# A top-k threshold search: its bits searched directly, and one secant search for four blocks instead of two for two

## The chip, the cores and the metric

One NeuronCore of a Trainium2 chip runs the whole program. The metric is device time in microseconds (us); the median of three runs is 2239.26 us. The engines are TensorE (PE: matmuls; PEld: its weight loads), VectorE (DVE), ScalarE (ACT), GpSimd (POOL) and the queue that issues nearly all DMAs (SP).

## The reference

A trunk of two layers over 2048 tokens of width 1024. The first layer has sparse attention beside a depthwise convolution of 31 taps; the second is a gated short convolution. What the change touches is the choice of keys in the sparse attention:

```python
for each block of 128 queries t:
    score = sum_h w[q, h] * relu(qi[q, h] . ki[s])      # 8 index heads
    score = where(s <= t, score, -inf)
    _, sel = top_k(score, 256)                          # 256 keys of each query
    p = softmax(q . k[sel] / 8 over valid sel);  out = p @ v[sel]
```

The kernel needs no list of the 256 keys. It needs, for each query row, a threshold such that 256 scores reach it; it then adds a mask of 0 or -1e30 to the logits.

## The kernel before, in words

The tokens are four chunks of 512 (numbered 0 to 3), and a chunk is four blocks of 128 queries (16 blocks in all, numbered 0 to 15). Block b has scores of width W = (b+1)*128. Blocks 0 and 1 need no search. A compile-time scheduler lays out each engine's instruction order; an engine then runs its list in that order. Program order is the scheduler's priority; `weave` mixes filler work (convolution, first attention) into matmul units.

Part one of the program runs, for each chunk c, `project(c)` (query and key projections), then `index` (the scores: TensorE into `ps_i`, ScalarE relu at L721, VectorE multiply-add into the score tile at L723, eight heads in columns of up to 1024), then the search. Between them lie `rest(c)` (the other projections and gates) as TensorE filler.

Blocks 2 and 3 (chunk 0) are searched exactly by `general`, called by `select_all`: 32 counts (L292) for each of the two blocks, one bit of the threshold at a time, with small VectorE operations on 128x2 tiles between them (L293 to L295, L301 to L304).

Chunks 1 to 3 use `select`, twice a chunk: blocks 0 and 1 of the chunk (pair A below) once their scores are there, then blocks 2 and 3 (pair B). `select` makes seven trips: ScalarE counts the scores above x (L774, one count a block), then a chain of ten small VectorE operations on 128x2 tiles (L778 to L789) moves x by the secant rule. Then the extraction: VectorE counts once more (L799), masks (L804), takes the best 16 scores below x (L730 to L732), picks the threshold (L812, L813) and writes the mask (L817). L821 notes rows that the search couldn't settle in `bad`.

The score tiles `sc0` to `sc3` have one buffer each, so `index` of block i of the next chunk waits until the extraction of block i of this chunk is done.

After chunk 3, `bad` is reduced to a flag (`fl`, L967; `fi`, L971), which every engine loads (L1133) ahead of an `If` that holds the exact search as a fallback, and that isn't taken here. Nothing that stands behind the `If` in the program can pass it: the rest of attention, the second layer. Ahead of it TensorE has `rest(3)`, the last gates (`last_gates`, tiles `yh`, `yl`) and the first output projection (`out_even`).

Of the kernel before, what the change touches and what calls it, by code (L numbers as in the profile page):

```python
# [12 lines left out]
FP32 = mybir.dt.float32  # L13
F16 = mybir.dt.float16
BF16 = mybir.dt.bfloat16
I32 = mybir.dt.int32
AF = mybir.ActivationFunctionType
ALU = mybir.AluOpType
# [3 lines left out]
P = 128  # L22
# [6 lines left out]
TT = CH // P  # L29
# [5 lines left out]
TOPK = 256  # L35
# [7 lines left out]
NCAND = 16  # L43
# [30 lines left out]
def trunk_kernel(ctx: ExitStack, tc: tile.TileContext, xT, pos, wE, woE, wO, woO, par, tab, outT):  # L74
    nc = tc.nc
    V, A, G, T, SP = nc.vector, nc.scalar, nc.gpsimd, nc.tensor, nc.sync
# [197 lines left out]
    def general(scs, get):  # L274
        bl = sorted(scs)
        nb, wmax = len(bl), (bl[-1] + 1) * P

        def small(name, dt=FP32):
            return get(name, TT, dt)[:, 0:nb]

        cur, tr, bits, xm, acc = small("cur", I32), small("try", I32), small("bits", I32), small("xm", I32), small("acc", I32)
        cnt, cg, tmp, zero, izero = small("cnt"), small("cg"), small("tmp"), small("zero"), small("izero", I32)
        V.memset(cg, 0.0)
        V.memset(zero, 0.0)
        V.memset(izero, 0)
        V.memset(xm, 0x7FFFFFFF)
        V.memset(cur, -2 ** 31)

        def count(th):
            for n, b in enumerate(bl):  # L290
                junk = get("junk", wmax, BF16)
                V.tensor_scalar(out=junk[:, 0:(b + 1) * P], in0=scs[b], scalar1=th[:, n:n + 1], scalar2=0.0, op0=ALU.is_ge, op1=ALU.add, accum_out=cnt[:, n:n + 1])  # L292
            V.tensor_scalar(out=acc, in0=cnt, scalar1=float(TOPK), scalar2=None, op0=ALU.is_ge)  # L293
            V.scalar_tensor_tensor(out=tmp, in0=cnt, scalar=float(TOPK), in1=cnt, op0=ALU.is_lt, op1=ALU.mult)
            V.tensor_tensor(out=cg, in0=cg, in1=tmp, op=ALU.max)  # L295

        count(zero)
        V.copy_predicated(out=cur, mask=acc, data=izero)
        V.copy_predicated(out=xm, mask=acc, data=izero)
        for bit in range(30, -1, -1):  # L300
            V.tensor_scalar(out=tr, in0=cur, scalar1=1 << bit, scalar2=None, op0=ALU.bitwise_or)  # L301
            V.tensor_tensor(out=bits, in0=tr, in1=xm, op=ALU.bitwise_xor)
            count(bits.bitcast(FP32))
            V.copy_predicated(out=cur, mask=acc, data=tr)  # L304
        V.tensor_tensor(out=bits, in0=cur, in1=xm, op=ALU.bitwise_xor)
        thr = bits.bitcast(FP32)
        V.tensor_scalar(out=cg, in0=cg, scalar1=-1.0, scalar2=float(TOPK), op0=ALU.mult, op1=ALU.add)
        for n, b in enumerate(bl):
            W = (b + 1) * P
            both, mb = get("eq", wmax, FP32), get("mb", wmax, BF16)[:, 0:W]  # L310
            eq, cs = both[:, 0:W], both[:, wmax:wmax + W]
            V.tensor_scalar(out=eq, in0=scs[b], scalar1=thr[:, n:n + 1], scalar2=None, op0=ALU.is_equal)
            V.tensor_tensor_scan(out=cs, data0=ones[:, 0:1].broadcast_to([P, W]), data1=eq, initial=0.0, op0=ALU.mult, op1=ALU.add)
            V.scalar_tensor_tensor(out=eq, in0=cs, scalar=cg[:, n:n + 1], in1=eq, op0=ALU.is_gt, op1=ALU.mult)
            V.scalar_tensor_tensor(out=eq, in0=scs[b], scalar=thr[:, n:n + 1], in1=eq, op0=ALU.is_lt, op1=ALU.add)
            V.tensor_scalar(out=mb, in0=eq, scalar1=NEG, scalar2=None, op0=ALU.mult)
            SP.dma_start(out=mb_dr[b], in_=mb)
# [90 lines left out]
    with ExitStack() as es:  # L408
# [6 lines left out]
        tk = es.enter_context(tc.tile_pool(name="tk", bufs=2))  # L415
# [285 lines left out]
        def index(c, qst, blocks):  # L701
            scs = {}
            first = cvp.tile([P, NJ, CH], FP32, name="cv") if c == 0 else None
            for i in blocks:
                b = c * TT + i
                W = (b + 1) * P
                if c == 0:
                    sc = first[:, i, 0:W]
                else:
                    sc = scp.tile([P, W], FP32, name=f"sc{i}", padded_shape=[P, (NB - TT + i + 1) * P])  # L710
                sm = tk.tile([P, 2], FP32, name=f"sm{i}")
                for sgi, s0 in enumerate(range(0, W, 1024)):
                    w = min(1024, W - s0)
                    for h in range(H):
                        ps = ps_i.tile([P, 1024], FP32, name="ps_i")
                        for r0 in range(0, w, 512):
                            r = min(512, w - r0)
                            for a in range(2):
                                T.matmul(out=ps[:, r0:r0 + r], lhsT=qst[:, h, i * P:(i + 1) * P], rhs=ki[:, a, s0 + r0:s0 + r0 + r], start=a == 0, stop=a == 1)  # L719
                        rl = e1.tile([P, 1024], FP32, name="relu")  # L720
                        A.activation(out=rl[:, 0:w], in_=ps[:, 0:w], func=AF.Relu)  # L721
                        kw = {"accum_out": sm[:, sgi:sgi + 1]} if h == H - 1 else {}
                        V.scalar_tensor_tensor(out=sc[:, s0:s0 + w], in0=rl[:, 0:w], scalar=wi[:, b, h:h + 1],  # L723
                                               in1=tiny[:, s0:s0 + w] if h == 0 else sc[:, s0:s0 + w],
                                               op0=ALU.mult, op1=ALU.add, **kw)
                scs[b] = (sc, sm, W)
            return scs
# [6 lines left out]
        def select(c, scs):  # L734
            bl = sorted(scs)
            nb, b0 = len(bl), bl[0]

            def small(name, dt=FP32, bufs=2):
                return tk.tile([P, 2], dt, name=name, bufs=bufs)[:, 0:nb]

            mu, sg, sq = small("t_mu"), small("t_sg"), small("t_sq")
            for n, b in enumerate(bl):
                sc, sm, W = scs[b]
                junk = tk.tile([P, S], BF16, name="junk", bufs=1)
# [24 lines left out]
            for it in range(NCOUNT):  # L769
                cn, d, t, xn = small("t_cn"), small("t_d", bufs=4), small("t_1"), small("t_x", bufs=4)  # L770
                for n, b in enumerate(bl):
                    sc, sm, W = scs[b]
                    junk = tk.tile([P, S], BF16, name="junk", bufs=1)
# [15 lines left out]
                V.tensor_tensor(out=xn, in0=x, in1=g if it > 0 else t, op=ALU.add)  # L789
                xl, dl, x = x, d, xn  # L790

            cand = tk.tile([P, 2, NCAND + 1], FP32, name="t_cand")
            cn, Tt, Tn, j, j1 = small("t_cn"), small("t_T"), small("t_Tn"), small("t_j"), small("t_j1")
            pick = tk.tile([P, NCAND + 1], FP32, name="t_pick")
            slot = tab_sb[:, TAB_IDX:TAB_IDX + NCAND + 1]
# [110 lines left out]
        acc = stats(0, held)  # L906
# [18 lines left out]

        def scan(c, xs):
            qst = project(c, xs)
            select(c, index(c, qst, (0, 1)))
            select(c, index(c, qst, (2, 3)))

        a, b, d = score_slot(3, 4), score_slot(0, 3), score_slot(1, 3)
        held = [a[:, k, :] for k in range(4)] + [b[:, k, :] for k in range(3)] + [d[:, 0, :]]
# [2 lines left out]
        acc = stats(1, held)  # L935
        state["gate"] = None
        qst = project(0, xs)
# [161 lines left out]
    def rows():  # L1099
        return l1.tile([P, KD, CH], FP32, name="x1"), l1.tile([P, CH], FP32, name="ssum", bufs=1)  # L1100
# [17 lines left out]
    x1, acc = rows()  # L1118
# [9 lines left out]
    n = norm_odd(x1, acc, late)  # L1128
# [4 lines left out]
    with tc.If(rv > 0):  # L1133
        with tc.tile_pool(name="fb", bufs=1) as fb:
            for c in range(1, NCH):
                scs = {}
                for i in range(TT):
                    b = c * TT + i
# [40 lines left out]
    for c in range(NCH):  # L1179
        att = attend(c + 1) if c + 1 < NCH else iter(())  # L1180
        if c > 0:
            cnv = conv(c + 1) if c + 1 < NCH else iter(())
            x1, acc = rows()
            weave(out_even(c, *m[c], x1, acc), 99, (cnv, CNR), (att, R0))
            n = norm_odd(x1, acc, late, (cnv, CNR), (att, R1))
# [78 lines left out]
```

## Time and profile before

| what | value |
|---|---|
| median of the runs shown (2239.11 to 2239.54) | 2239.26 us |
| the profiled execution | 2238.43 us |
| its span in the trace | 2236.6 us |
| TensorE busy in the span | 1992.6 us (89%) |
| VectorE busy | 1677.2 us (75%) |
| ScalarE busy | 1119.3 us (50%) |
| GpSimd busy | 773.8 us (35%) |

The profiled execution is 1.8 us longer than its span. Times in the trace count from the start of the span. A matmul's record is longer than the step from one matmul to the next, since matmuls overlap in the array; the busy figures count overlapping records once.

### The profile page before, as it was taken

What the parts mean: (1) busy time and instruction counts of PE and PEld (TensorE: products, weight loads), DVE (VectorE), ACT (ScalarE), POOL (GpSimd) and SP (SyncE); (2) the same over time, 40 slices, a digit from 0 to 9 for tenths busy, and PEclk for the clock granted to TensorE, in tenths of its full rate; (3) what the DMA queues carried; (4) which work ended last, traced back from release to release, by engine and by line L of the source; (5) the groups of instructions that cost most, each with busy time, mean ns of one, the idle gap of its engine ahead of it and who ended that gap; (6) DMA issues with size and microseconds to landing.
All of it is one profiled execution on the core that took longest, in us unless ns stands there. A gap on an engine that the chain in (4) does not pass through costs nothing.

```text
span 2236.6 us, 34187 instructions
## 1 busy us (share of the span) xinstructions
PE 1992.6 (89%) x12252; PEld 1070.5 (48%) x12252; DVE 1677.2 (75%) x3568; ACT 1119.3 (50%) x1899; POOL 773.8 (35%) x633
## 2 busy tenths in 40 slices
PE   5777888988999898798889998989998989999997
PEld 4544464555454543344444444544554444444446
DVE  7999979999887876778875899763899874243224
ACT  5556655567568756366664553451555463121111
POOL 4755343534142502246552543430444442000000
PEclk9989999999999998899989999999999999999999
DMA  6445456334744466678886787773778976324224
GB/s 237 160 157 192 164 172 228 111 115 139 222 127 151 130 227 212 205 208 206 199 211 190 174 202 188 179 182 121 184 173 190 207 159 162 118 101 147 96 97 167
DMA packets 408094, 380.85 MB, mean 170 GB/s; under 512 B 315504, under 2 KB 335728, under 8 KB 387184
## 3 DMA queue, kind: packets, MB, share of 16 engines
q1 hardware_dynamic: 407920, 378.64, 59.5%
q8 instruction: 96, 1.57, 0.3%
q14 instruction: 78, 0.64, 0.1%
HBM read 216.45 MB, written 88.70 MB: 136 GB/s over the span
## 4 chain that ended last, share of the span: by engine, by line
PE 24%; DVE 13%; DMA 8%; issue 5%; ACT 4%; POOL 3%; SPq 1%; POOLq 0%; DVEq 0%; ACTq 0%
PE ps_w L189 7%; PE ps_w L188 7%; PE ps_w L187 7%; DVE lg L340 3%; DVE ps_c L241 3%; DMA w_stage<-in_wo_dram 2%; DMA pth<-ph 2%; POOL pl L351 2%; DMA ptl<-pl 1%; ACT ph L350 1%; DMA cin<-cg_dr 1%; DVE y L1060 1%; ACT lg L343 1%; POOL wt L210 1%; DVE nl L183 1%
## 5 line engine op out<-in xcount | busy, mean ns | idle before, releaser
L351 POOL TENSOR_TENSOR pl<-lg,ph 128x1024 f16<-128x1024 f32 (+7 forms) x192 | 317.1, 1664 | 562.3 <-ACT ph L350 444.5
L187 PE MATMUL ps_w<-nh,wt 128*128 128x512 f16 x1024 | 389.1, 382 | 6.8 <-ACT wt L209 4.6
L189 PE MATMUL ps_w<-nh,wt 128*128 128x512 f16 x1024 | 388.4, 382 | 3.6 <-POOL wt L210 3.5
L188 PE MATMUL ps_w<-nl,wt 128*128 128x512 f16 x1024 | 390.1, 382 | 1.4 <-DVE nl L183 1.4
L187 PEld LDWEIGHTS <-wt 128*128 128x128 f16 x2112 | 208.6, 99 | 258.7 <-issue 24.1
L189 PEld LDWEIGHTS <-wt 128*128 128x128 f16 x2112 | 208.8, 99 | 245.3 <-issue 16.0
L188 PEld LDWEIGHTS <-wt 128*128 128x128 f16 x2112 | 209.0, 99 | 242.4 <-issue 27.3
L241 DVE SCALAR_TENSOR_TENSOR ps_c<-cin,cwt,ps_c 128x512 f32<-128x512 f32 x348 | 260.2, 748 | 20.1 <-ACT ps_c L239 17.1
L210 POOL TENSOR_TENSOR wt<-w_stage,wt 128x512 f16<-128x512 f32 x136 | 167.9, 1241 | 285.8 <-ACT wt L209 260.5
L343 ACT ACTIVATE lg<-lg,m 128x128 f32<-128x128 f32 (+15 forms) x128 | 153.5, 1199 | 136.7 <-DVE m L340 132.1
L187 PE MATMUL ps_p<-xh,wt 128*128 128x512 f16 x480 | 186.2, 389 | 16.3 <-ACT th L222 4.5
L350 ACT CAST ph<-lg 128x1024 f16<-128x1024 f32 (+7 forms) x192 | 148.2, 792 | 95.1 <-DMA pth<-ph 93.4
L189 PE MATMUL ps_p<-xh,wt 128*128 128x512 f16 x480 | 185.7, 389 | 2.1 <-POOL wt L210 2.1
L188 PE MATMUL ps_p<-xl,wt 128*128 128x512 f16 x480 | 186.1, 388 | 0.0
L721 ACT ACTIVATE relu<-ps_i 128x1024 f32<-128x1024 f32 (+7 forms) x176 | 140.9, 811 | 75.5 <-DVE sc L723 42.8
L723 DVE SCALAR_TENSOR_TENSOR sc<-relu,wi,sc 128x1024 f32<-128x1024 f32 (+7 forms) x140 | 162.3, 1160 | 13.2 <-ACT relu L721 12.4
L719 PE MATMUL ps_i<-ki,qst 128*128 128x512 f16 (+3 forms) x608 | 145.3, 361 | 26.7 <-ACT relu L721 26.3
L187 PE MATMUL ps_p<-wt,xh 128*128 128x256 f16 (+1 forms) x608 | 164.8, 271 | 4.6 <-ACT u L578 2.4
L188 PE MATMUL ps_p<-wt,xh 128*128 128x256 f16 (+1 forms) x608 | 164.6, 271 | 0.6 <-POOL wt L210 0.6
L189 PE MATMUL ps_p<-wt,xl 128*128 128x256 f16 (+1 forms) x608 | 163.9, 271 | 1.2 <-DVE xl L473 1.2
L1156 PE MATMUL ps_q<-kk,qs_a 128*128 128x512 f16 (+3 forms) x576 | 146.8, 356 | 12.2 <-DVE m L340 11.9
L774 ACT ACTIVATE junk<-sc,t_x 128x640 bf16<-128x640 f32 (+5 forms) x84 | 118.7, 1413 | 58.1 <-DVE t_x L789 34.2
(294 smaller groups left out, 3989.8 us busy)
## 6 DMA issues: line engine op xcount, KB each, us to landing
wt<-w_in_wo_dram SPq DMA_DIRECT2D x48, 1024.0 KB, 5.0
wt<-w_in_we_dram SPq DMA_DIRECT2D x39, 1024.0 KB, 5.4
w_stage<-in_wo_dram SPq DMA_DIRECT2D x64, 256.0 KB, 3.3
w_in_wo_dram<-wt SPq DMA_DIRECT2D x16, 1024.0 KB, 4.9
wt<-w_in_woo_dram SPq DMA_DIRECT2D x16, 1024.0 KB, 4.8
w_in_we_dram<-wt SPq DMA_DIRECT2D x13, 1024.0 KB, 4.8
w_stage<-in_we_dram SPq DMA_DIRECT2D x48, 256.0 KB, 3.4
wt<-w_in_woe_dram SPq DMA_DIRECT2D x12, 1024.0 KB, 4.8
```

What stands on the lines that cost most here:

```text
L187: T.matmul(out=out, lhsT=sh(k), rhs=mh(k), start=k == 0, stop=False)
L188: T.matmul(out=out, lhsT=sh(k), rhs=ml(k), start=False, stop=False)
L189: state["mm"] = T.matmul(out=out, lhsT=sl(k), rhs=mh(k), start=False, stop=k == KD - 1)
L210: G.tensor_tensor(out=wt[:, 1, ks, :], in0=st, in1=wt[:, 0, ks, :], op=ALU.subtract)
L241: ins = V.scalar_tensor_tensor(out=out if t == CK - 1 else acc, in0=ci[:, t:t + CH], scalar=cwt[:, j, t:t + 1], in1=acc, op0=ALU.mult, op1 ...
L343: A.activation(out=lg[:, 0:W], in_=lg[:, 0:W], func=AF.Exp, bias=last, scale=-1.0, accum_out=ss[:, h:h + 1])
L350: A.copy(out=ph, in_=e)
L351: eng.tensor_tensor(out=pl, in0=e, in1=ph, op=ALU.subtract)
L719: T.matmul(out=ps[:, r0:r0 + r], lhsT=qst[:, h, i * P:(i + 1) * P], rhs=ki[:, a, s0 + r0:s0 + r0 + r], start=a == 0, stop=a == 1)
L721: A.activation(out=rl[:, 0:w], in_=ps[:, 0:w], func=AF.Relu)
L723: V.scalar_tensor_tensor(out=sc[:, s0:s0 + w], in0=rl[:, 0:w], scalar=wi[:, b, h:h + 1], in1=tiny[:, s0:s0 + w] if h == 0 else sc[:, s0:s0 ...
L1156: ins = T.matmul(out=ps[:, 0:w], lhsT=qs[:, h, :], rhs=kk[:, a, s0:s0 + w], start=a == 0, stop=a == 1)
```

## The change

`general`: the threshold's own bits are searched. `cur` starts at all ones (or at zero where 256 scores are at least zero), and each bit is flipped by an exclusive-or, so that the operation that turned bits into a number (L302) goes. The running maximum of counts below 256 (L294, L295, after every count) goes too; one count with "greater than" at the end gives it instead.

`select`: it is called once a chunk with all four blocks. Its small tiles are four columns wide instead of two, and `t_cand` has one buffer instead of two.

```diff
-            V.scalar_tensor_tensor(out=tmp, in0=cnt, scalar=float(TOPK), in1=cnt, op0=ALU.is_lt, op1=ALU.mult)
-            V.tensor_tensor(out=cg, in0=cg, in1=tmp, op=ALU.max)
-        count(zero)
-        V.copy_predicated(out=cur, mask=acc, data=izero)
-        V.copy_predicated(out=xm, mask=acc, data=izero)
+            V.copy_predicated(out=cur, mask=acc, data=data)
+        count(zero, cnt, ALU.is_ge)
+        keep(izero)
         for bit in range(30, -1, -1):
-            V.tensor_scalar(out=tr, in0=cur, scalar1=1 << bit, scalar2=None, op0=ALU.bitwise_or)
-            V.tensor_tensor(out=bits, in0=tr, in1=xm, op=ALU.bitwise_xor)
-            count(bits.bitcast(FP32))
-            V.copy_predicated(out=cur, mask=acc, data=tr)
-        V.tensor_tensor(out=bits, in0=cur, in1=xm, op=ALU.bitwise_xor)
-        thr = bits.bitcast(FP32)
+            V.tensor_scalar(out=tr, in0=cur, scalar1=1 << bit, scalar2=None, op0=ALU.bitwise_xor)
+            count(tr.bitcast(FP32), cnt, ALU.is_ge)
+            keep(tr)
+        thr = cur.bitcast(FP32)
+        count(thr, cg, ALU.is_gt)
...
-                return tk.tile([P, 2], dt, name=name, bufs=bufs)[:, 0:nb]
+                return tk.tile([P, TT], dt, name=name, bufs=bufs)[:, 0:nb]
...
-            cand = tk.tile([P, 2, NCAND + 1], FP32, name="t_cand")
+            cand = tk.tile([P, TT, NCAND + 1], FP32, name="t_cand", bufs=1)
...
             qst = project(c, xs)
-            select(c, index(c, qst, (0, 1)))
-            select(c, index(c, qst, (2, 3)))
+            select(c, index(c, qst, range(TT)))
```

## Rows read from the trace of the kernel before

**Rows 1.** The page's first part: engines, busy time and share.
```profile
PE 1992.6 (89%) x12252; PEld 1070.5 (48%) x12252; DVE 1677.2 (75%) x3568; ACT 1119.3 (50%) x1899; POOL 773.8 (35%) x633
```
**Rows 2.** Windows by stage: stretch, its length, then busy us of each engine.
```profile
100.00:283.00 183.00, 146.96 (x897) 85.67 (x896) 176.94 (x526) 115.16 (x213) 93.67 (x94) 0.92 0.49 169
...
587.00:799.00 212.00, 193.34 (x1212) 108.87 (x1211) 178.76 (x389) 154.68 (x233) 67.92 (x67) 1.00 0.49 142
...
820.00:868.00 48.00, 36.87 (x157) 15.74 (x155) 13.77 (x72) 38.05 (x46) 4.58 (x4) 0.86 0.70 241
868.00:926.00 58.00, 54.64 (x256) 24.58 (x254) 53.56 (x87) 24.35 (x42) 19.73 (x16) 1.00 0.57 193
```
**Rows 3.** Waits of TensorE, 100 to 283 us: total, times, longest.
```profile
PE ps_t L613 <- DVE stk L600: 14.6, 4, 5.6
...
PE ps_t L613 <- DVE stk L606: 3.2, 3, 2.4
```
**Rows 4.** Timeline of VectorE at the flag: start, us, instruction, idle before.
```profile
925.25 0.16 DVE L967 TENSOR_REDUCE fl<-bad 128x1 f32<-128x16 f32 x1
...
933.75 0.45 DVE L147 TENSOR_TENSOR rs_t<-rs_r 128x4 f32<-128x4 f32 x1 [5.17 <-DVEq L1133]
```
**Rows 5.** Waits of TensorE, 926 to 940 us.
```profile
PE ps_m L169 <- DVE rs_d L163: 10.1, 1, 10.1
```
**Rows 6.** Groups by line, whole span: xcount, busy us, mean ns, idle before.
```profile
L292 DVE TENSOR_SCALAR_CACHE_REDUCE mk<-cv,s_bits 128x384 bf16<-128x384 f32 (+1 forms) x62 | 41.9, 676 | 1.1
...
L781 DVE SCALAR_TENSOR_TENSOR t_d<-t,t_d 128x2 f32<-128x2 f32 x42 | 12.6, 301 | 0.8
...
L302 DVE TENSOR_TENSOR s_bits<-s_try,s_xm 128x2 int32<-128x2 int32 x31 | 8.8, 285 | 0.5
...
L294 DVE SCALAR_TENSOR_TENSOR s_tmp<-s_cnt 128x2 f32<-128x2 f32 x32 | 7.9, 247 | 0.0
L295 DVE TENSOR_TENSOR s_cg<-s_cg,s_tmp 128x2 f32<-128x2 f32 x32 | 7.8, 242 | 0.0
...
L785 DVE RECIPROCAL t_g<-t_g 128x2 f32<-128x2 f32 x36 | 5.8, 162 | 0.7
```
**Rows 7.** Groups by line on VectorE, 820 to 868 us, the last search.
```profile
L780 DVE TENSOR_TENSOR t<-t_d 128x2 f32<-128x2 f32 x7 | 1.1, 161 | 0.2
```
**Rows 8.** Groups by line and shape on ScalarE, whole span: the counts.
```profile
L774 ACT ACTIVATION_READ_ACCUMULATOR junk<-sc,t_x 128x1 f32 x84 | 15.9, 189 | 0.0
L774 ACT ACTIVATE junk<-sc,t_x 128x2048 bf16<-128x2048 f32 x7 | 14.0, 1998 | 0.1
...
L774 ACT ACTIVATE junk<-sc,t_x 128x1152 bf16<-128x1152 f32 x7 | 8.8, 1252 | 6.9 <-DVE t_x L764 4.1 <-DVE t_x L789 2.7
```
**Rows 9.** Timeline of VectorE: the slot of block 8 freed, block 12 begun.
```profile
585.29 0.81 DVE L817 TENSOR_SCALAR mb<-sc,t_T 128x1152 bf16<-128x1152 f32 x1
...
587.09 1.27 DVE L723 SCALAR_TENSOR_TENSOR sc<-relu,wi,tiny 128x1024 f32<-128x1024 f32 x1
```
**Rows 10.** Windows of L723 alone: the multiply-adds of chunks 2 and 3.
```profile
346.00:522.00 176.00, 65.67 (x71) 0.95 0.43 138
...
587.00:799.00 212.00, 78.85 (x72) 1.00 0.49 142
```
**Rows 11.** Groups by line, 587 to 799 us, ScalarE: the counts among the index work.
```profile
L774 ACT ACTIVATE junk<-sc,t_x 128x1408 bf16<-128x1408 f32 (+3 forms) x28 | 45.5, 1626 | 20.5 <-DVE t_x L789 12.7 <-DVE t_x L764 5.3 <-DVE rs_t L148 2.4
```
**Rows 12.** The same stretch on VectorE: two of ten search lines.
```profile
L787 DVE TENSOR_TENSOR t_g<-t_g,t_gmin 128x2 f32<-128x2 f32 x12 | 5.1, 427 | 0.2
...
L785 DVE RECIPROCAL t_g<-t_g 128x2 f32<-128x2 f32 x12 | 1.9, 162 | 0.3
```
**Rows 13.** Groups by line on VectorE, 868 to 926 us: work beside the last extraction.
```profile
L241 DVE SCALAR_TENSOR_TENSOR ps_c<-cin,cwt,ps_c 128x512 f32<-128x512 f32 x23 | 17.1, 744 | 0.0
...
L1016 DVE SCALAR_TENSOR_TENSOR x<-ps_w,xi 128x512 f32<-128x512 f32 x8 | 5.4, 676 | 4.4 <-DMA xi<-in_x_dram 4.4
L179 DVE TENSOR_TENSOR ssum<-ssum,sq 128x512 f32<-128x512 f32 x7 | 5.1, 723 | 0.0
```

More of the change, by code (lines that the diff above doesn't have):

```diff
@@ L279, in small @@
             return get(name, TT, dt)[:, 0:nb]
-        cur, tr, bits, xm, acc = small("cur", I32), small("try", I32), small("bits", I32), small("xm", I32), small("acc", I32)
-        cnt, cg, tmp, zero, izero = small("cnt"), small("cg"), small("tmp"), small("zero"), small("izero", I32)
-        V.memset(cg, 0.0)
+        cur, tr, acc = small("cur", I32), small("try", I32), small("acc", I32)
+        cnt, cg, zero, izero = small("cnt"), small("cg"), small("zero"), small("izero", I32)
         V.memset(zero, 0.0)
@@ L285, in general, with count @@
         V.memset(izero, 0)
-        V.memset(xm, 0x7FFFFFFF)
-        V.memset(cur, -2 ** 31)
-        def count(th):
+        V.memset(cur, -1)
+        def count(th, out, op):
             for n, b in enumerate(bl):
                 junk = get("junk", wmax, BF16)
-                V.tensor_scalar(out=junk[:, 0:(b + 1) * P], in0=scs[b], scalar1=th[:, n:n + 1], scalar2=0.0, op0=ALU.is_ge, op1=ALU.add, accum_out=cnt[:, n:n + 1])
+                V.tensor_scalar(out=junk[:, 0:(b + 1) * P], in0=scs[b], scalar1=th[:, n:n + 1], scalar2=0.0, op0=op, op1=ALU.add, accum_out=out[:, n:n + 1])
@@ L293, in count, with keep @@
+        def keep(data):
             V.tensor_scalar(out=acc, in0=cnt, scalar1=float(TOPK), scalar2=None, op0=ALU.is_ge)
-            V.scalar_tensor_tensor(out=tmp, in0=cnt, scalar=float(TOPK), in1=cnt, op0=ALU.is_lt, op1=ALU.mult)
-            V.tensor_tensor(out=cg, in0=cg, in1=tmp, op=ALU.max)
-        count(zero)
-        V.copy_predicated(out=cur, mask=acc, data=izero)
-        V.copy_predicated(out=xm, mask=acc, data=izero)
-        for bit in range(30, -1, -1):
-            V.tensor_scalar(out=tr, in0=cur, scalar1=1 << bit, scalar2=None, op0=ALU.bitwise_or)
-            V.tensor_tensor(out=bits, in0=tr, in1=xm, op=ALU.bitwise_xor)
-            count(bits.bitcast(FP32))
-            V.copy_predicated(out=cur, mask=acc, data=tr)
```

## The prediction

> **What bounds the kernel now.** I read the page's busy shares first, then windows by stage, the waits of TensorE in each, and timelines where a wait ends. TensorE is busy 89% of the span, VectorE 75% [rows 1]; the mean hides two stages. From 100 to 283 us, where the exact search runs, VectorE is busy 177 of 183 us and TensorE 147 of 183 [rows 2]: VectorE is full, and TensorE waits for VectorE's `stk` tiles, 14.6 + 3.2 = 17.8 us [rows 3]. The second place is the `If`. The flag is reduced at 925.25 us; VectorE then stands 5.17 us on loading it (L1133) in the middle of a row norm, and TensorE stands 10.1 us behind that norm [rows 4, 5]. Two chains end there together: TensorE's list of work ahead of the `If` (done about 926 us, where those 10.1 us of wait begin) and the search of chunk 3. Whichever is later sets when all that follows starts, and nothing behind the `If` reads a threshold in another way than before. So the forecast is for two numbers: when TensorE is done with its list (P, now 926), and when the flag is there (F, now 925).
>
> **The exact search.** Each of 31 bits loses L302, L294 and L295. By their means that is 285 + 247 + 242 = 774 ns, 24.0 us in all [rows 6]. But the same kind of operation on a 128x2 tile takes 161 ns [rows 7] where GpSimd is nearly idle, 4.58 of 48 us [rows 2], so part of the mean is waiting for something, and a wait can fall on the next operation instead. At 161 ns the 93 removed are worth 15.0 us. The two counts added at the end (2 x 0.68 us) [rows 6] are paid by what goes outside the loop (three more of the same small operations, a predicated copy, two memsets). So VectorE is relieved of 15 to 24 us of 177.
>
> The Trainium skill (SBUF — State Buffer, "Who interferes with whom") says that a VectorE instruction with two SBUF inputs, or a `tensor_scalar` in a two-port mode, is locked out for the whole of a GpSimd instruction that holds the shared port. The rows agree: 161 ns against 242 to 285. By that rule the wait passes to the next small operation and the saving is near 15 us; by the means it is 24.
>
> For TensorE this is worth at most the 17.8 us that it waits there for `stk`, and at least nothing (its list is filled with `rest(0)`, which is the cover; if that is gone, the whole relief counts). The four long waits lie spread over the search, so on average half of the relief lies ahead of them: half of 15 to 24, I take 9 us.
>
> **The secant search, operations.** The ten chain lines run 42 or 36 times in six searches, from 12.6 us (L781) down to 5.8 us (L785), 93.7 us in sum [rows 6]. Three searches instead of six halve that: 47 us less on VectorE, and some 13 us less of set-up (about 17 small operations for each search saved, at L294's mean). Four columns instead of two I cost at nothing; the bound above, twice 161 ns for each of 70 operations, is 11 us a search. Little of this 60 us stands before TensorE: it is hidden under matmuls of `rest` as long as P is not held by it. I credit P with nothing for it.
>
> **The secant search, order.** This is where the change can lose. Pair A's seven trips now run while pair B's scores are made, and pair B's extraction while the next chunk's scores begin. After the change the trips start when the last of four blocks has its scores, and the next chunk waits for the first free slot: today block 12 starts 1.8 us after the mask of block 8 is begun (587.09 against 585.29) [rows 9]. I follow the chain to F.
>
> - Scores of chunk 2: done at 522 now [rows 10]. 9 us earlier by the above, and without small operations of a search among them some 8 us more: 505.
> - Search of its four blocks: counts grow evenly from 1.25 us (W=1152) to 2.00 us (W=2048) over eight widths [rows 8]; four of chunk 2 are 5.65 us, their accumulator reads 0.76, the chain ten operations of 0.16 and their gaps, 1.9. Seven trips are 58 us. The last pair's 48 us [rows 2] against 43 by the same sum gives a factor 1.1; I take 70 (58 to 81). Set-up 5, extraction up to the first free slot 28 (a pair's share, 25, to 35): block 12 starts at 608 (590 to 635) instead of 587.
> - Scores of chunk 3: 212 us now, for 78.9 us of multiply-adds [rows 10]. What goes from among them: 45.5 us of counts on ScalarE, which stand in the queue before the relus [rows 11], the chain (1.9 to 5.1 us a line, ten lines, 32 us) [rows 12], and pair A's extraction, about 20 us by the last pair's. VectorE's 178.8 us [rows 2] become 127. I take 145 us, a little above that (130 to 160): done at 753 instead of 799 (720 to 795).
> - From there to the flag: 127 us now (799 to 926). Search: 7 x (7.35 + 0.76 + 1.9) = 70, times 1.1 is 77 instead of 48: +29. Extraction: in 868 to 926 VectorE is busy 53.6 us, of which 27.6 are convolution and projection [rows 2, 13], so two blocks cost 26, and two narrower ones +24. Set-up no longer shares VectorE with pair A's extraction: -11. The convolution can move into VectorE's idle time in the search (13.8 of 48 us busy) [rows 2]: -12 (0 to -25). Sum 157 (144 to 169): F at 910 (864 to 964).
>
> So both chains get shorter or stay: P = 926 - 9 = 917 and F = 910. P decides, and with the flag there before TensorE is done, some of the 10.1 us behind the norm goes as well; I take 3. The profiled execution would take 2238.4 - 9 - 3 = 2226.4 us; the median stands 0.8 us above the profiled execution, so I forecast 2227 us. What is late next is TensorE's own list.
>
> **Rivals.** *The flag is late (slower).* If index work doesn't speed up when the counts leave, because its pace is set by hand-over between the engines, chunk 3's scores take the 176 us that chunk 2's took [rows 10]. F = 608 + 176 + 157 = 941, 15 us late with TensorE idle: 2254 us, and 2281 us with the late bound for block 12 (635). For it: VectorE was busy only 178.8 of 212 us in chunk 3, with ScalarE at 154.7 [rows 2], so neither was full. Against it: the counts are in the relus' own queue. It decides from the point where chunk 3's scores end later than about 770. The Trainium skill (Perfetto Trace Analysis, "Optimization Strategy") recommends interleaving stages that press on different engines; the change takes such an interleaving apart. By that rule the time is this rival's, and the trace agrees with it so far: VectorE is 13.8 of 48 us busy while a search runs alone [rows 2].
>
> *Nothing comes of it (same).* F ties at 926, or the 9 us at the exact search are lost in TensorE's next wait: 2238 to 2240 us. For it: TensorE has the highest share, 89%, so a relief of VectorE may go to idle time. The Trainium skill (Perfetto Trace Analysis, "Identifying the Most-Contended Engine") tells to optimize the engine with the highest occupancy first. By that rule the time stays.
>
> *The change doesn't do what it says.* The scheduler might put the four-block tiles so that blocks wait for a buffer anyway; the time is then between the two above. Nothing in the rows speaks for it.
>
> **How the numbers follow.** What a measurement can tell from no change is 0.2%, 4.5 us. Forecast (P decides, 2215 to 2234 us): 0.47. Late flag: 0.31. Nothing: 0.19. Not as it says: 0.03, split. So faster 0.48, same 0.20, slower 0.32. The lower end of the range takes all 17.8 us of `stk` waits and most of the 10.1 us at the `If`: 2212. Above I go to 2260, which holds the late flag up to a delay of 21 us; beyond lies about 0.12, below 0.05.
>
> **What would show it.** L302, L294 and L295's busy time gone, with 15 us less or 24 on VectorE between 100 and 283; the wait for `stk` there below 17.8 us. Ten chain lines 18 or 21 times, near 47 us in sum. The first multiply-add of block 12 near 608 us, the last of block 15 near 753, L967 near 910 and TensorE's last matmul before the norm's wait near 917. The forecast is wrong if L967 stands later than TensorE's list by more than some 10 us, if block 15's scores end after 770, or if TensorE's waits of before 283 us only move to other lines.

## The result, and the profile after

The changed kernel takes 2255.75 us (median of 5, 2248.05 to 2259.18) against 2239.54 us for the kernel before in the same runs, 16 us slower by the medians; the ratio over all runs is 1.0063 with a 95% interval of [1.0039, 1.0087]. The forecast was 2227 us. The time lies inside the range, but on the other side of no change.

The page's first part of the changed kernel, to be read against [rows 1]:

```profile
PE 1995.6 (88%) x12252; PEld 1072.1 (47%) x12252; DVE 1632.3 (72%) x3212; ACT 1127.8 (50%) x1901; POOL 779.9 (35%) x633
```

VectorE has 45 us less to do and 356 instructions fewer. So work did go; the time was lost elsewhere. Windows by stage (columns as in [rows 2]) show where to look: the exact search, the scores of chunk 3, its search, its extraction, and the stretch behind the flag.

```profile
100.00:283.00 183.00, 149.29 (x922) 87.60 (x921) 173.00 (x409) 120.18 (x218) 100.34 (x99) 0.94 0.53 184
...
637.00:817.00 180.00, 168.59 (x976) 88.67 (x975) 128.78 (x186) 107.83 (x157) 51.49 (x45) 1.00 0.55 155
817.00:921.00 104.00, 83.97 (x364) 36.14 (x363) 47.71 (x134) 83.78 (x114) 23.42 (x21) 0.92 0.56 196
921.00:1027.00 106.00, 87.76 (x368) 37.58 (x368) 104.03 (x164) 49.02 (x88) 36.68 (x29) 0.90 0.50 176
1030.00:1130.00 100.00, 80.93 (x533) 40.56 (x532) 79.98 (x171) 66.77 (x123) 55.86 (x42) 0.98 0.86 214
1130.00:1230.00 100.00, 75.67 (x495) 40.06 (x494) 67.52 (x126) 57.70 (x98) 46.70 (x28) 0.85 0.80 194
```

The timeline of VectorE gives the chain to the flag: slot freed and block 12 begun (the pair of [rows 9]), last multiply-add of block 15, flag (the rows of [rows 4]), first attention of chunk 1 (L337), first row of `out_even` of chunk 1 (L1012).

```profile
635.52 0.81 DVE L814 TENSOR_SCALAR mb<-sc,t_T 128x1152 bf16<-128x1152 f32 x1
...
637.39 1.74 DVE L720 SCALAR_TENSOR_TENSOR sc<-relu,wi,tiny 128x1024 f32<-128x1024 f32 x1
...
815.38 1.28 DVE L720 SCALAR_TENSOR_TENSOR sc<-relu,wi,sc 128x1024 f32<-128x1024 f32 x1 [3.03 <-ACT relu L718]
...
1026.59 0.15 DVE L963 TENSOR_REDUCE fl<-bad 128x1 f32<-128x16 f32 x1
1026.66 0.73 DVE L1056 SCALAR_TENSOR_TENSOR y<-cx,par_sb,y 128x512 f32<-128x512 f32 x1
...
1029.56 0.68 DVE L1060 SCALAR_TENSOR_TENSOR y<-ps_w,y 128x512 f32<-128x512 f32 x1
...
1030.81 0.15 DVE L967 TENSOR_SCALAR fi<-ps_m 128x1 int32<-128x1 f32 x1
1034.90 0.69 DVE L1064 SCALAR_TENSOR_TENSOR th<-th,ps_w 128x512 f32<-128x512 f32 x1 [3.94 <-DVEq L1129]
...
1042.51 0.69 DVE L337 CUSTOM_DVE_ANT_0 lg<-ps_q,mb_a 128x512 f32<-128x512 f32 x1 [0.20 <-DMA ga_a<-ga_dr]
...
1222.19 0.69 DVE L1012 SCALAR_TENSOR_TENSOR x<-ps_w,xi 128x512 f32<-128x512 f32 x1 [7.69 <-PE ps_w L189]
```

The flag is 101 us later than before (925.25), and 117 us later than forecast (910). Yet the last row, 1222.19, comes only 19 us later than before (1203.38 in the trace of before), and the whole run is 21 us longer in the profiled execution. L1056 and L1060 say why: they are the second layer's first projection, `odd`, which stands behind the `If` in the program, and here they run ahead of it. TensorE's work for it shows in the windows of `ps_w` (the second layer's matmuls) between 926 and 1030 us, after and, in the second fence, before:

```profile
926.00:1030.00 104.00, 90.76 (x381) 7.18 (x11) 4.14 (x7) 0.92 0.49 171
```

```profile
926.00:1030.00 104.00, 68.46 (x291) 6.17 (x9) 4.12 (x7) 0.93 0.71 202
```

The compile-time scheduler had laid 381 of these matmuls into TensorE's list in that stretch, while the flag was awaited; in the kernel before, where the flag is there at 925 us, the stretch holds 291 beside the attention of chunk 1. So the sentence that nothing behind the `If` can pass it, on which the forecast and its late-flag rival both stood, is false for this program. What did wait is the attention of chunk 1.

### The profile page after: what moved, and what is told of

It reads as the page before. It is cut to its first block, busy times and chain, and to the rows that moved or that the text cites. A ratio compares the mean times of both kernels' runs of the same rounds, so it can differ in the third digit from the quotient of the medians.

```text
span 2257.4 us, 33870 instructions
## 1 busy us (share of the span) xinstructions
PE 1995.6 (88%) x12252; PEld 1072.1 (47%) x12252; DVE 1632.3 (72%) x3212; ACT 1127.8 (50%) x1901; POOL 779.9 (35%) x633
## 4 chain that ended last, share of the span: by engine, by line
PE 26%; DVE 11%; DMA 7%; issue 3%; ACT 3%; POOL 2%; SPq 1%; DVEq 0%; ACTq 0%; POOLq 0%
PE ps_w L187 8%; PE ps_w L189 8%; PE ps_w L188 8%; DMA pth<-ph 3%; DVE lg L337 3%; DVE ps_c L241 3%; POOL pl L348 2%; PE ps_q L1152 1%; ACT ph L347 1%; PE ps_v L370 1%; DMA ptl<-pl 1%; DMA w_stage<-in_wo_dram 1%; DMA w_stage<-in_woo_dram 1%; ACT lg L340 1%; DVE y L1056 1%
## 5 line engine op out<-in xcount | busy, mean ns | idle before, releaser
L188 PE MATMUL ps_w<-nl,wt 128*128 128x512 f16 x1024 | 392.8, 384 | 4.7 <-DVE nl L183 4.7
L188 PEld LDWEIGHTS <-wt 128*128 128x128 f16 x2112 | 208.9, 99 | 248.2 <-issue 32.5
L720 DVE SCALAR_TENSOR_TENSOR sc<-relu,wi,sc 128x1024 f32<-128x1024 f32 (+7 forms) x140 | 168.7, 1205 | 34.2 <-ACT relu L718 33.1
L188 PE MATMUL ps_p<-xl,wt 128*128 128x512 f16 x480 | 184.1, 384 | 0.7 <-DMA xl<-xs_dr 0.7
L188 PE MATMUL ps_p<-wt,xh 128*128 128x256 f16 (+1 forms) x608 | 164.6, 271 | 0.3 <-POOL wt L210 0.3
L370 PE MATMUL ps_v<-vv,pth 128*128 128x128 f16 x1008 | 112.8, 223 | 25.6 <-DMA pth<-ph 22.7
```

The costliest lines, as they stand in the source:

```text
L188: T.matmul(out=out, lhsT=sh(k), rhs=ml(k), start=False, stop=False)
```

## The experiments

Times of the table are starts of rows in each profiled execution: VectorE's first and last multiply-add of chunk 3's scores, the flag, TensorE's first row of the attention of chunk 1, VectorE's first row of `out_even` of chunk 1. Each ratio is to the kernel before in the same runs (medians 2239.54 to 2241.30 us) with its 95% interval; it is taken over all runs and is not the quotient of the two medians.

| kernel | median us | ratio to before | scores of chunk 3 | flag | attention 1 | out_even 1 |
|---|---|---|---|---|---|---|
| before | 2239.54 | 1 | 587.1 to 797.4 | 925.2 | 952.0 | 1203.4 |
| changed | 2255.75 | 1.0063 [1.0039, 1.0087] | 637.4 to 815.4 | 1026.6 | 1041.9 | 1222.2 |
| search_only | 2233.76 | 0.9977 [0.9967, 0.9987] | 568.2 to 780.3 | 906.3 | 939.9 | 1189.5 |
| four_only | 2276.47 | 1.0161 [1.0146, 1.0175] | 652.1 to 836.6 | 1054.9 | 1067.6 | 1239.1 |
| four_12 | 2240.47 | 1.0000 [0.9990, 1.0010] | 636.8 to 827.6 | 944.9 | 958.8 | 1204.1 |
| four_3 | 2244.58 | 1.0020 [1.0008, 1.0033] | 569.7 to 754.7 | 938.9 | 954.7 | 1202.0 |
| late_flag | 2243.21 | 1.0010 [1.0000, 1.0019] | 587.1 to 797.4 | 1010.4 | 1026.0 | 1205.0 |
| late_flag_more | 2275.78 | 1.0156 [1.0143, 1.0170] | 587.3 to 797.5 | 1061.3 | 1076.7 | 1236.1 |
| before_no_if | 2224.72 | 0.9924 [0.9911, 0.9937] | 587.0 to 797.4 | 925.7 | 948.8 | 1185.3 |
| after_no_if | 2250.48 | 1.0037 [1.0025, 1.0049] | 636.3 to 813.6 | 1025.2 | 1029.6 | 1211.6 |
| four_first | 2263.24 | 1.0093 [1.0078, 1.0107] | 636.3 to 810.2 | 997.7 | 1016.1 | 1222.8 |
| four_bare | 2333.56 | 1.0425 [1.0410, 1.0440] | 621.1 to 713.2 | 892.6 | 1056.1 | 1295.8 |
| search_31 | 2237.23 | 0.9991 [0.9978, 1.0005] | 568.3 to 775.2 | 920.0 | 942.8 | 1196.0 |
| search_31_all | 2245.96 | 1.0017 [1.0005, 1.0030] | 605.0 to 784.0 | 934.5 | 949.4 | 1203.7 |

**Which half costs.** `search_only` has the new `general` with the old `select` (its tiles and buffers as before, too); `four_only` the reverse.

```diff
 # search_only
-            select(c, index(c, qst, range(TT)))
+            select(c, index(c, qst, (0, 1)))
+            select(c, index(c, qst, (2, 3)))
```

> Only the exact search of the change (bits searched directly, one count above at the end); chunks 1 to 3 still search two blocks at a time. Theory (the loss comes from the flag, which the four-block search makes about 100 us late): the flag stays within 15 us of the 925 us of before, TensorE's stk waits between 100 and 283 us stay near 15 us, and the time is 2230 to 2242 us. Rival (the exact search's edit costs by itself, because it lets the scheduler lay out the first 300 us another way): 2248 us or more.

> Only the four-block secant search of the change; the exact search is that of before. Theory (late flag): the flag at 1010 to 1045 us, attention of chunk 1 begins after it and is done close to 1215 us without matmuls beside it at its end, 2250 to 2262 us. Rival (the exact search's edit costs): the time of before within 5 us, 2235 to 2244 us.

`search_only` gains 0.23%; its flag is 19 us earlier, a little more than expected. `four_only` loses 1.61%, with a flag at 1054.9 us; both are more than expected. The exact search is a gain, the four-block search is the whole loss, and under the four-block search the exact search is worth more (1.0161 to 1.0063) than alone: a first sign that the price of a late flag is not a straight line.

**Which chunk.** The four-block search in chunks 1 and 2 only, and in chunk 3 only; the four columns of the tiles and the one buffer of `t_cand` stay throughout.

```diff
 # four_12 (four_3: c == NCH - 1)
-            select(c, index(c, qst, range(TT)))
+            if c < NCH - 1:
+                select(c, index(c, qst, range(TT)))
+            else:
+                select(c, index(c, qst, (0, 1)))
+                select(c, index(c, qst, (2, 3)))
```

> The change, but chunk 3 is searched two blocks at a time; chunks 1 and 2 keep the four-block search. Theory (late flag, made up of a late start of chunk 3's scores and a long way from its last score to the flag): chunk 3's scores begin near 637 us as in the changed kernel, and the flag comes 338 us after that as before, at about 975 us, half as late; attention of chunk 1 keeps some of its cover, 2238 to 2250 us. Rival (only chunk 3's own search matters): flag near 925 us and 2232 to 2240 us.

> The change, but chunks 1 and 2 are searched two blocks at a time; only chunk 3 uses the four-block search. Theory (late flag): chunk 3's scores begin near 587 us, its flag comes 390 us after that as in the changed kernel, at about 977 us, 2238 to 2250 us. Rival (only chunk 3's own search matters): flag at 1015 us or later and 2250 to 2260 us. Rival of both (the lateness has no price, the loss lies in chunks 1 and 2): 2232 to 2240 us.

The flags come at 945 and 939 us, not near 976 as expected: 39 and 33 us behind that of `search_only`. And neither costs more than 0.2% against the kernel before, though 0.2 and 0.4% against `search_only`. The rival that only chunk 3's own search matters falls. In `four_12` the scores of chunk 3 begin 69 us later than in `search_only` and the flag is 39 us later: part is won back, in the scores (191 instead of 212 us) and behind them (117 instead of 126 us, so the one buffer of `t_cand` shows no cost there). In `four_3` the scores take 185 instead of 212 us once the counts are not among them, and all of that and 31 us more is lost again between the last score and the flag (184 against 126 us).

From these runs I took it that a late flag is paid at about a quarter of its lateness. Their waits of TensorE (905 to 945 us) show another cost, which I overlooked. First `four_3`, then `four_12`:

```profile
PE ps_m L169 <- DVE t_pick L810: 21.6, 1, 21.6
```

```profile
PE ps_m L169 <- DVE t_pick L809: 16.7, 1, 16.7
```

L169 is the row norm's matmul; it waits 2.5 us in `search_only`, and 22.7 us in `four_first` below. The norm's few small operations on VectorE, from L160 to L163, take 17 us in `four_3` and 15 us in `four_12`, against 2.5 us in `search_only`, because steps of the extraction and the convolution stand between them in VectorE's list. The norm's first row (L1036; L1033 in `search_only`) then comes at 939.3 and 943.6 us instead of 920.9, and `out_even` of chunk 1 is 13 and 15 us later than there. So the flag need not be what these two pay for.

The next run held back the flag alone.

**The flag alone.** In the kernel before, the result of the last search goes through turns of two small copies before it is reduced. The turns change no value.

```diff
+        turns = [const.tile([P, NB], FP32, name=f"turn{k}") for k in range(2)]
+        held_bad = bad
+        for n in range(80):          # late_flag_more: 130
+            A.copy(out=turns[0], in_=held_bad)
+            G.tensor_copy(out=turns[1], in_=turns[0])
+            held_bad = turns[1]
-        V.tensor_reduce(out=fl, in_=bad, axis=mybir.AxisListType.X, op=ALU.max)
+        V.tensor_reduce(out=fl, in_=held_bad, axis=mybir.AxisListType.X, op=ALU.max)
```

> The kernel before, with nothing of the change. Between the result of the last search and the flag stand 80 turns of a copy of 128x16 on ScalarE and one on GpSimd, each waiting for the other, so that only the flag comes late (how late is read from its row; about 60 to 110 us). Theory (a late flag is paid at about a quarter of its lateness up to 100 us, because the second layer's first projection runs ahead of the branch, and more steeply beyond): for a flag 100 us late 2256 to 2266 us. Rival (a late flag costs nothing, since TensorE has other work; the loss comes from the longer VectorE and ScalarE work of the four-block search itself): 2238 to 2246 us. Rival from the prediction (every microsecond of lateness past TensorE's list is lost): 2300 us or more.

> As late_flag (the kernel before, only the flag held back), with 130 turns instead of 80, so that the flag is later than in the changed kernel, near 1060 us. The runs so far put the start of out_even of chunk 1 at the later of two chains: TensorE's own work (about 1203 us) and attention of chunk 1, which takes some 180 us once it begins, about 14 us behind the flag. Theory (two chains; the price is nothing up to a flag near 1010 us, then one for one): for a flag at 1060 us out_even of chunk 1 begins near 1254 us and the time is 2280 to 2296 us. Rival (a flag alone is cheap; what costs in the changed kernel is the extraction's VectorE work standing in the second layer's): 2243 to 2256 us.

With the flag 85 us late the time rises by 0.10%: the quarter price was wrong, and this run alone would have spoken for the rival. (The flag's load is gone from the row norm here, whose first row comes at 932.8 instead of 938.5 us, so some 6 us of a price may be hidden.) With the flag 136 us late it rises by 1.56%, which that rival excludes (and it is less than one for one: `out_even` of chunk 1 begins at 1236, not 1254). So, against the kernel before, a late flag costs next to nothing up to about 1010 us and then, over the next 51 us, 1.46% of the time, some 33 us. The rows of `late_flag_more`:

```profile
1061.30 0.17 DVE L973 TENSOR_REDUCE fl<-turn 128x1 f32<-128x16 f32 x1
...
1077.82 0.69 DVE L340 CUSTOM_DVE_ANT_0 lg<-ps_q,mb_a 128x512 f32<-128x512 f32 x1 [4.71 <-PE ps_q L1162]
...
1236.09 0.69 DVE L1022 SCALAR_TENSOR_TENSOR x<-ps_w,xi 128x512 f32<-128x512 f32 x1 [7.17 <-PE ps_w L189]
```

A straight line between these two ratios gives, at the changed kernel's flag of 1026.6 us, 1.0010 + 0.0146 x 16.2 / 50.9 = 1.0056; measured were 1.0063 [1.0039, 1.0087]. At the flag of `four_only` it gives 1.0138; measured were 1.0161 [1.0146, 1.0175]. By this line lateness alone, with none of the change, accounts for the loss against the kernel before within some 0.2%. That the price runs straight between the two points is assumed; no run holds the flag back to a time between them. And the changed kernel also has the exact search's gain, 0.23% alone, so some 0.3% more than the line may have to be explained. A candidate, not tested, is TensorE's wait for the second layer's rows, which stand among the extraction on VectorE (groups by line, 926 to 1030 us, after and, in the second fence, before):

```profile
L187 PE MATMUL ps_w<-nh,wt 128*128 128x512 f16 x127 | 50.2, 401 | 16.3 <-ACT nh L182 9.1 <-DVE y L1060 6.6 <-DVE cx L1051 0.4
```

```profile
L187 PE MATMUL ps_w<-nh,wt 128*128 128x512 f16 x97 | 37.0, 392 | 2.0 <-ACT nh L182 1.5 <-ACT cs L1051 0.5
```

**The branch itself.** The `If` and the fallback in it are left out (rows that the secant search can't settle are then not searched exactly).

```diff
-    rv = nc.values_load(fi[0:1, 0:1], min_val=0, max_val=1)
-    with tc.If(rv > 0):
...
-                general(scs, lambda n, w, dt: fb.tile([P, 2 * w if n == "eq" else w], dt, name=f"f_{n}"))
```

> The kernel before without the branch and the fallback in it (the exact search that runs where the flag is set is left out). Theory (the flag at 925 us stands on the path at a quarter of its lateness and VectorE's 5 us load of it in the row norm too): attention of chunk 1 begins before 950 us, 2226 to 2237 us. Rival (attention waits for the memory of the score tiles or for its masks, not for the branch): within 4 us of the kernel before.

> The changed kernel without the branch and the fallback in it (the exact search that runs where the flag is set is left out). Theory (what waits is the loads of attention, which stand behind the branch on SP's queue): attention of chunk 1 begins well before 1020 us, while the last extraction still runs, and the time falls to 2225 to 2240 us. Rival (attention needs the memory that the score tiles of chunk 3 give back, so it can't start before the last mask at about 1020 us anyway): attention begins after 1015 us and the time stays within 6 us of the changed kernel.

In the changed kernel attention of chunk 1 still begins only at 1029.6 us, behind the last mask of chunk 3 at 1018.5 us: the first theory falls, and the rival holds, in that without the branch attention still begins only behind the end of chunk 3's search. Whether it is the score tiles' memory, the masks or the order of SP's queue that makes it wait was not told apart. The branch adds 12 us to that start, and leaving it out is worth about a quarter of a per cent. In the kernel before it is worth 0.76% (2224.72 against 2241.30 us in the same runs, 16.6 us), just beyond the range that was expected. Of these, 6 us stand at the row norm (its first row is at 932.5 instead of 938.5 us), and 18 us in sum by the start of `out_even` of chunk 1; where the other 12 come from wasn't tried.

**What sets the pace of the scores.** `four_first` raises the priority of chunk 3's index and search; `four_bare` forbids the projections that stand behind chunk 3's search to be placed ahead of its last score matmul.

```diff
 # four_first, in scan
+            if c == NCH - 1:
+                with tc.high_priority(PRI):
+                    select(c, index(c, qst, range(TT)))
 # four_bare: at the first matmul of each projection between scan(3) and rest(3)
+            if k == 0 and state.get("hold") is not None:
+                tc.add_manual_dep(first.ins, state["hold"].ins.name, ...)   # hold: chunk 3's last score matmul
```

> The changed kernel with the index work and the search of chunk 3 given the scheduler's high priority, so that TensorE's list holds fewer other matmuls between those of the scores. Theory (the pace of chunk 3's scores, 180 us, is set by the other matmuls in TensorE's order, 119 of these 180 us): the scores take 110 to 150 us, the flag comes 30 us or more earlier than 1027 us, and the time falls by 5 to 15 us. Rival (the pace is set by the hand-over from ScalarE to VectorE): the scores take 165 us or more and the time stays within 4 us of the changed kernel.

> The changed kernel, but the projections of the chunks that stand in the program behind chunk 3's search may not be placed ahead of the last score matmul of chunk 3 in TensorE's order. Theory (the pace of chunk 3's scores is set by the other matmuls between them): the scores take 90 to 140 us instead of 180, and the flag comes 30 us or more earlier; what the whole time does depends on whether the projections then fit beside the search (2235 to 2265 us). Rival (the hand-over from ScalarE to VectorE sets the pace): the scores take 165 us or more, the flag stays at 1010 us or later, and TensorE loses time: 2270 us or more.

`four_first` tells nothing on the pace, because the edit did not do its work: the same projections still stand between the scores (133 matmuls of L188 with 512 columns, 138 without the edit), and the scores take 174 us. The flag comes 29 us earlier all the same, and the time gets longer, not shorter: TensorE is busy 76.0 of the 104 us from 926 instead of 90.8, and the row norm's first row is at 941.0 instead of 925.0 us, behind the 22.7 us of wait named above.

`four_bare` does take them out, and the scores take 92 instead of 178 us. The windows and the groups by line of that stretch:

```profile
621.00:714.00 93.00, 63.97 (x255) 25.56 (x255) 86.41 (x111) 62.73 (x68) 0.89 (x3) 0.90 0.11 45
```

```profile
L718 PE MATMUL ps_i<-ki,qst 128*128 128x512 f16 x240 | 61.1, 383 | 65.6 <-ACT relu L720 65.1
```

VectorE is now full (86.4 of 93 us), and TensorE waits 26 us for it by way of ScalarE: of the 65.1 us in the row, one wait of 39.0 us ends at TensorE's first score at 623.5 us and lies nearly all ahead of this stretch. In the changed kernel it was the other way round (groups by line, 637 to 817 us): TensorE is busy 168.6 of 180 us, 55.6 of them with scores, and most of the rest is projections in its fixed order.

```profile
L716 PE MATMUL ps_i<-ki,qst 128*128 128x512 f16 x240 | 55.6, 357 | 7.5 <-ACT relu L718 7.3
L188 PE MATMUL ps_p<-xl,wt 128*128 128x512 f16 x138 | 52.3, 379 | 0.0
...
```

The flag of `four_bare` is 134 us earlier than in the changed kernel, and the kernel is 4.25% slower than before, far above the 2265 us that the theory allowed: the projections that had filled TensorE during the scores, and would have filled the 39 us of wait ahead of them, now stand ahead of the first `out_even` (its first row is at 988.2 instead of 860.1 us). An early flag is worth little if TensorE pays for it.

**A shorter way from the last score to the flag.** The new exact search, and in chunk 3 (or in chunks 1 to 3) three blocks and then one alone; the small tiles are three columns wide. The edit is shown against `search_only`.

```diff
 # search_31 (search_31_all: in every chunk)
-            select(c, index(c, qst, (0, 1)))
-            select(c, index(c, qst, (2, 3)))
+            for blocks in ((0, 1, 2), (3,)) if c == NCH - 1 else ((0, 1), (2, 3)):
+                select(c, index(c, qst, blocks))
```

> The new exact search, secant search by two blocks in chunks 1 and 2, and in chunk 3 three blocks and then the last one alone, so that the work behind the last score gets shorter (one block's counts and extraction instead of two). Theory (two chains; ahead of the flag TensorE's list decides, and with the new exact search it is done near 908 us): the flag comes 15 to 35 us earlier than the 906 us of the new exact search with pairs, and since TensorE's list decides then, the time gains 0 to 6 us on it: 2226 to 2235 us. Rival (searching three blocks together holds up the scores of the last one, so the flag is no earlier): 2232 to 2242 us.

> As search_31, with three blocks and then one in chunks 1 and 2 too. Theory (the next chunk's scores begin when the first slot is free; three blocks are searched while the fourth's scores are made): chunk 3's scores begin between the 568 us of pairs and the 637 us of four blocks, near 575 us, and the flag within 15 us of search_31's; 2226 to 2238 us. Rival (every block more in a search delays the first free slot in full): chunk 3's scores begin after 600 us and the time is 2236 to 2246 us.

Both theories missed: the flag is later than with pairs (920.0 and 934.5 against 906.3 us), and `search_31_all` begins the scores of chunk 3 at 605 us. Neither beats `search_only`, which is the fastest version here with the fallback in it.

## Why the prediction was wrong, step by step

**The exact search: right on VectorE, in its size too; on TensorE the size came, but not from the wait that was named.** The three lines are gone. Of the six small lines of a bit three are left (groups by line, whole span, to be read against [rows 6]):

```profile
L293 DVE TENSOR_SCALAR s_acc<-s_cnt 128x2 int32<-128x2 f32 x32 | 12.9, 402 | 0.3
L299 DVE TENSOR_SCALAR s_try<-s_cur 128x2 int32<-128x2 int32 x31 | 10.8, 347 | 0.7
L294 DVE COPY_PREDICATED s_cur<-s_acc,s_try 128x2 int32<-128x2 int32 x31 | 10.3, 332 | 0.6
```

In the trace of before the six were 54.0 us; the three are 34.0: 20 us less, between the 15 and 24 of the forecast. The three that stay took 334, 280 and 327 ns before and take 402, 347 and 332 now, so part of the wait passed to the neighbours. The Trainium skill (SBUF — State Buffer, "Who interferes with whom") says that whoever meets a locked port waits for the whole of the other's instruction; the trace agrees in that part of the wait moves, and 20 us lies about midway between the two sums. That the wait is one for this port no run here shows.

TensorE's gain of 9 us came: its list ends, at the wait for the norm, at 917 us in the changed kernel and in `search_only` (forecast 917), against 926, and VectorE's last row of the first `out_even` is at 906.7 and 908.4 us against 917.1. But it did not come out of the waits that I took it from, and that step of the prediction failed; they are still there, 16.6 us of 17.8 [rows 3]:

```profile
PE ps_t L610 <- DVE stk L597: 14.5, 7, 4.7
...
PE ps_t L610 <- DVE stk L603: 2.1, 3, 1.3
```

Where it came from instead I have not traced, so the 9 us were right by luck, as far as is known. One clue: behind the exact search, from 283 to 350 us, TensorE ran 452 matmuls in `search_only` instead of 415, at a mean granted clock of 1.00 instead of 0.92. The rival by which the relief would come to nothing falls with `search_only` (0.9977). The Trainium skill (Perfetto Trace Analysis, "Identifying the Most-Contended Engine"), which the prediction names for that rival, judges TensorE by other figures than its matmul busy time, so its rule did not speak for it by the 89%.

**The chain of small operations: right.** Its ten lines are 46 us in sum (forecast 47). VectorE as a whole has only 45 us less than before, not the sum of what these lines and the exact search lost: its busy time counts overlapping rows once, and some other lines took longer (the multiply-adds of L720, for one, 83.1 us in chunk 3 instead of 78.9).

**The way to the flag: wrong, by 117 us, in three terms.** Scores of chunk 2 end at 504.9 us (forecast 505), and then:

| term | forecast | measured |
|---|---|---|
| end of chunk 2's scores to block 12 | 103 | 132.5 |
| scores of chunk 3 | 145 | 178 |
| last score to flag | 157 | 211 |

*The scores of chunk 3*, 33 us. The step that failed is that VectorE's and ScalarE's lists set their pace, so that taking the counts and the chain away would speed them up. VectorE's work there did fall to 128.8 us (forecast 127), and the scores took 178 us all the same. TensorE was busy 193.3 of 212 us there [rows 2], and I did not count it. `four_bare` shows the pace to be that of the other matmuls in TensorE's order: 92 us without them. The 32 us that were won go with a shorter list: TensorE had 141 us of `ps_p` projections among the scores before (587 to 799 us) and 119 in the changed kernel (637 to 817 us). The 176 us of the late-flag rival came close, but not by the hand-over between engines that it named.

*The set-up of the search*, costed at 5 us. In chunk 2 it took 21 us, from the last score at 504.9 us to the first count at 525.6. (The rest of that term's excess is the search, 78 us against 70, and the extraction up to block 12, 34 against 28.) No row gave the 5 us: before, the last set-up already took 23 us, from 797.4 to 820.1 us. The timeline of VectorE shows the small operations of one dependent chain, and between most of them a convolution step, here of 1.2 to 1.3 us:

```profile
507.12 0.25 DVE L751 TENSOR_TENSOR t<-t_mu 128x4 f32<-128x4 f32 x1
507.29 0.14 DVE L747 TENSOR_SCALAR t_sq<-t_sq 128x1 f32<-128x1 f32 x1
507.35 1.18 DVE L241 SCALAR_TENSOR_TENSOR cv<-cin,cwt,cv 128x512 f32<-128x512 f32 x1
508.46 0.68 DVE L752 TENSOR_TENSOR t_sq<-t_sq,t 128x4 f32<-128x4 f32 x1
509.06 1.29 DVE L241 SCALAR_TENSOR_TENSOR cv<-cin,cwt,cv 128x512 f32<-128x512 f32 x1
510.27 0.68 DVE L753 TENSOR_SCALAR t_sq<-t_sq 128x4 f32<-128x4 f32 x1
510.87 1.29 DVE L241 SCALAR_TENSOR_TENSOR cv<-cin,cwt,cv 128x512 f32<-128x512 f32 x1
512.08 0.69 DVE L144 TENSOR_SCALAR vr_r<-t_sq 128x4 int32<-128x4 int32 x1
```

The filler stands between them in VectorE's list, so a chain that hops through this list pays one filler step per hop. The 13 us that I credited to saved set-ups never reached this chain: it is 16 us longer than I had put it.

*Search and extraction of chunk 3.* From the first count (822.0) to the first extraction count (921.1) it is 99 us, forecast 77: ScalarE is busy 83.8 of 104 us there (the windows above), and 23.0 of them are casts of weights (L208 and L209) that stand among the counts. The extraction to the flag is 105 us, forecast 70 (58 + 24 - 12): VectorE is full, 104.0 of 106 us, and among its groups by line the convolution, which I had moved into the search, stands first, followed by the extraction and then by the second layer's rows that ran ahead of the `If` (L1056, L1032):

```profile
L241 DVE SCALAR_TENSOR_TENSOR ps_c<-cin,cwt,ps_c 128x512 f32<-128x512 f32 x31 | 22.9, 739 | 1.3 <-ACT ps_c L239 1.3
L801 DVE SCALAR_TENSOR_TENSOR mk<-mb,sc 128x1024 f32<-128x1024 bf16 (+3 forms) x8 | 10.8, 1352 | 0.0
...
L1056 DVE SCALAR_TENSOR_TENSOR y<-cx,par_sb,y 128x512 f32<-128x512 f32 x8 | 7.0, 869 | 0.0
L1032 DVE SCALAR_TENSOR_TENSOR xi<-x,par_sb,ps_m 128x512 f32<-128x512 f32 x8 | 5.6, 738 | 0.0
```

**What a late flag costs: wrong as well.** The late-flag rival had its deciding point right (chunk 3's scores past 770 us; they end at 815) and its time, 2254 us, is the one measured, but by luck: it priced 15 us of lateness one for one. In fact the flag was 101 us late, and in `late_flag` 85 us cost 0.10%, while `odd` ran ahead of the branch there too (373 `ps_w` matmuls from 926 to 1030 us). What is then late is the attention of chunk 1. It stands bare at its end, as the windows of the changed kernel and its waits of TensorE from 1030 to 1225 us show:

```profile
1190.00:1210.00 20.00, 7.36 (x86) 5.59 (x84) 12.33 (x20) 8.78 (x17) 5.55 (x3) 0.64 1.01 259
```

```profile
PE ps_v L370 <- DMA pth<-ph: 16.5, 7, 5.1
```

From the start of that attention to `out_even` of chunk 1 it is 251 us before, 180 in the changed kernel, 179 in `late_flag`, 172 in `four_only` and 159 in `late_flag_more`. So it shrinks as its start comes later, but here not below some 160 to 180 us, and from about there lateness is paid. Why it can still shrink from 180 to 159 wasn't tried. TensorE had 7.4 of 20 us of work from 1190 us on, and the mean granted clock was 0.64, between its two levels (1.2 and 2.4 GHz); in the 20 us ahead it was 0.83 with 14.2 us of work, and 1.00 with 18.8 us in the 20 us before those.

The Trainium skill (Perfetto Trace Analysis, "Optimization Strategy") recommends interleaving stages that press on different engines. The runs agree: taking the pair interleaving apart costs 1.61% (`four_only`), and taking the projections out of the scores brings the changed kernel from 1.0063 to 1.0425 (`four_bare`).

## What to carry to other kernels

Before crediting a stage with the work taken from one engine, look at the busy share of the others in that same stage: where TensorE fills a stage to 91% with its own list, relieving VectorE gives little as long as that list stays as long. A flag or branch that comes late has a slack, set by the work that the scheduler can lay ahead of it; measure that slack by holding back the one event alone, at two latenesses or more, before pricing anything by it. A short chain of small operations can be the dear part of a longer extraction, where the two share one engine's list: here the row norm. And a batch of two made into one of four saves small operations but loses the overlap of one half's search with the other half's scores.

## What had not been expected of the hardware and its lists

An `If` that is never entered, with the fallback in it, costs 0.76% here (2224.72 us without it, 16.6 us less), of which only 6 us show where VectorE stands on the flag's load. By itself: the Trainium skill (Runtime: NRT & Kernel Launch, "Instruction fetch mechanics") says that a taken branch to a page outside the window has to fetch it first; no run here shows whether that is part of the 16.6 us.
